# Strided attention on one core: stores of one head parity from every second partition, for two groups at a time

## The chip, the cores and the metric

The kernel runs on one core of a Trainium2 chip. The metric is the device time in microseconds (us), the median over several executions. The profile is one further execution; its instruction times count from the start of its span.

## The reference

Inputs Q, K, V are fp32 of shape (8, 12, 1024, 64): batch, heads, sequence, head dimension. Every query attends to only 16 keys, the positions 0, 64, 128 ... 960.

```python
attend_positions = np.arange(0, seq, stride)          # stride 64: 16 positions
scores = einsum('bhqd,bhkd->bhqk', q, K[:, :, attend_positions]) / sqrt(dim)
weights = exp(scores - max(scores)); weights /= sum(weights) + 1e-10
result = einsum('bhqk,bhkd->bhqd', weights, V[:, :, attend_positions])
```

The output has the shape of V. So Q (25.2 MB) is read once, the output (25.2 MB) is written once, and little else moves.

## The kernel before, in words

The 96 heads are cut into 24 groups of four heads. A group is 1 MiB of Q and 1 MiB of output. All DMA transfers are issued on SP's queue by the helper `_copy` (L26 to L41); nearly every one therefore carries the line L35.

Loads. `load(g)` brings a group of Q into a tile `qn` of 128 partitions with 8 KiB each (32 query rows of one head). The first two groups are read as 128 rows of 8 KiB, all later ones as 32 rows of 32 KiB (L93 to L96). There are QBUFS = 8 such tiles, so eight loads are issued at the start, with K and V among them.

Work on one group `g`, spread over the engines and over several turns of the main loop:

- `cast` (L199, POOL): Q to bf16, three groups ahead.
- `transpose` (L203, DVE): 32 by 32 blocks of 4-byte pairs, two groups ahead.
- `scores` (L210, PE): four matmuls into one PSUM bank of 128 partitions by 512; then two exps on ACT (L221) write the weights into `w`, 64 partitions each. A head parity `a` (0 or 1) has its keys on 64 of the partitions and its queries in half of the 128 columns of each of the eight blocks of `w`; the other half of its columns stays zero from a memset at the start. One group ahead.
- `values` (L191, POOL): the values of the group's keys, spread by a mask, with four columns that make the sums of the weights.
- `outputs(g, c)` in three parts of 3, 2 and 3 blocks (L235, PE): each matmul takes one block of `w` as its weights, so a column of `w` becomes a partition of the output. DVE takes the reciprocal of the sums (L243); parts of 3 blocks are scaled by DVE (L245), the part of 2 is copied by ACT (L247) and scaled by POOL (L248). They write the tile `out_sb`, 128 partitions of 8 KiB. There are OBUFS = 9 of them.
- `store(g)`: one transfer, 128 reads of 8 KiB, each written as two pieces of 4 KiB.

The layout of `out_sb` before: partitions 0 to 63 hold the even heads of the group, partitions 64 to 127 the odd ones. Each partition holds 16 query rows of each of two heads, and row j of the 128 goes to byte offset 4096 j of the group for one head pair, and 512 KiB further on for the other.

Order. The program is written out by hand (a manual schedule; each engine keeps the order of the program text). In turn g of the main loop come `ahead(g)`, the three `outputs`, now and then a piece of preparing keys and values, then `store(g)` and `load(g + 8)`. SP goes through its queue in order: a store waits for the group's last writes to `out_sb`, and the load behind it waits with it. A transfer is counted on one of eight DMA semaphores in turn, and before a transfer is issued SP also waits until the one eight places earlier on the queue has landed. A tile `out_sb` is written again only when the stores that read it have landed; a tile `qn` is loaded again only when its cast is done.

Of the kernel before, what the change touches and what calls it, by code (L numbers as in the profile page):

```python
# [11 lines left out]
FP32 = mybir.dt.float32  # L12
# [7 lines left out]
def _ap_with(ap: bass.AP, new_ap, extra_offset: int = 0) -> bass.AP:  # L20
    return dataclasses.replace(
        ap, ap=[list(p) for p in new_ap], offset=ap.offset + extra_offset
    )


def _copy(nc, out: bass.AP, in_: bass.AP):  # L26

    sides = [
        mybir.BassSymbolicTensorAccessPattern(
            ap=side.ap, dtype=side.dtype, bass_ap=side,  # L30
            is_dma=True, for_custom_bir_dma=True,
        )
        for side in (in_, out)
    ]
    return nc.sync.add_instruction(  # L35
        mybir.InstDMACopy(
            name=nc.get_next_instruction_name(), engine=mybir.EngineType.SP,
            ins=sides[:1], outs=sides[1:], queue="qSPDynamicHW",
            mode="Copy",
        )  # L40
    )  # L41
# [9 lines left out]
def kernel(  # L51
# [10 lines left out]
    B, H, S, D = Q.shape  # L62
# [3 lines left out]
    P = 128  # L66
    HG = 4
    NG = B * H // HG
    NC = NG // 2
    SD = S * D  # L70
    KW = P + NK
    assert B * H == NG * HG and S == 1024 and D == 64 and NK == 16
    QBUFS = 8
    OBUFS = 9

    const = ctx.enter_context(tc.tile_pool(name="const", bufs=1))
    qn_pool = ctx.enter_context(tc.tile_pool(name="qn", bufs=QBUFS))
    out_pool = ctx.enter_context(tc.tile_pool(name="outsb", bufs=OBUFS))
    qb_pool = ctx.enter_context(tc.tile_pool(name="qb", bufs=2))
# [13 lines left out]
    def load(g):  # L93
        qn[g] = qn_pool.tile([P, 32 * D], FP32, name="qn", tag="qn")
        n = P if g < 2 else 32
        _copy(nc, qn[g], _ap_with(Q, [[HG * SD // n, n], [1, HG * SD // n]], g * HG * SD))  # L96
# [3 lines left out]
    nc.sync.dma_start(v_raw, _ap_with(V, kv_src))  # L100
    for g in range(1, QBUFS):
        load(g)
# [12 lines left out]
    for c in range(2):  # L115
        for a in range(2):
            for e in range(2):
                nc.gpsimd.tensor_copy(  # L118
                    out=perm_v[:, c, a, :, e], in_=id_v[:, c, :, a]
# [5 lines left out]
    for i in range(3):  # L125
# [7 lines left out]
        out=slot_i, in0=iota_p, scalar1=4, scalar2=3,  # L133
# [6 lines left out]
        out=s_sel, in0=col4, scalar1=slot_f, scalar2=None, op0=ALU.is_equal  # L140
# [15 lines left out]
    def key_rows(m):  # L156
        part = slice(4 * m, 4 * m + 4)
        nc.scalar.copy(k_bf[:, part], k_raw[:, part])  # L158
        nc.vector.transpose(  # L159
            k_r[:, part].rearrange("p n d -> p (n d)").bitcast(I32),  # L160
            k_bf[:, part].rearrange("p n d -> p (n d)").bitcast(I32),
        )


    def keys(m, c):
        for s in range(4):
            src, dst, col = 32 * (2 * c + s % 2), 32 * (2 * (s % 2) + s // 2), NK + 32 * s
            op = nc.vector.tensor_copy if m == 0 and s >= 2 else nc.scalar.copy
            op(  # L169
                k_t[dst : dst + 32, 8 * m + c : 8 * m + 8 : 2, :, col : col + NK],  # L170
                k_r[src : src + 32, 4 * m : 4 * m + 4].rearrange(
                    "p n (a k f) -> p a n f k", a=2, f=2
                )[:, s // 2],
            )


    def value_rows(n):
        for c in range(2):
            vp = psum_sc.tile([P, NC // 2, D], FP32, name="vp", tag="sc")
            nc.tensor.matmul(  # L180
                vp, lhsT=perm_v[:, c].rearrange("p a b e k -> p (a b e k)"),
                rhs=v_bf[:, 6 * n : 6 * n + 6], start=True, stop=True,
            )
            nc.vector.tensor_copy(out=v_rep[:, 6 * n : 6 * n + 6, c], in_=vp)  # L184

    qb, qt, wt, vb, rec, out_sb = {}, {}, {}, {}, {}, {}


    def values(g):
# [15 lines left out]
    def scores(g):  # L205
        sc = psum_sc.tile([P, 512], FP32, name="sc", tag="sc")
        q = qt[g]
        for e in range(2):
            for f in range(2):
                nc.tensor.matmul(  # L210
                    sc, lhsT=k_t[:, g, f, NK * (1 - e) : NK * (1 - e) + P],
                    rhs=_ap_with(
                        q, [q.ap[0], [D, 8], [16 * D, 2], [2, 32]],
                        extra_offset=8 * D * e + f,
                    ),
                    start=e + f == 0, stop=e + f == 2,
                )
        w = wt[g] = w_bufs[g % 3]
        for a in range(2):
            wa = w[64 * a : 64 * a + 64]  # L220
            nc.scalar.activation(  # L221
                out=_ap_with(wa, [wa.ap[0], [P, 8], [1, 2], [2, 32]], extra_offset=64 * a),
                in_=sc[64 * a : 64 * a + 64].rearrange("p (t x q) -> p t x q", t=8, x=2),
                func=AF.Exp, bias=0.0, scale=scale,
            )


    def outputs(g, c):
        if c == 0:
            out_sb[g] = out_pool.tile([P, 4, 8, D], FP32, name="out_sb", tag="out_sb")  # L230
            rec[g] = rec_pool.tile([P, 8, 4], FP32, name="rec", tag="rec")
        i0, n = ((0, 3), (3, 2), (5, 3))[c]
        ps = psum_o.tile([P, 3, 512], FP32, name="o_ps", tag="o")
        for i in range(n):
            nc.tensor.matmul(  # L235
                ps[:, i, 0 : 4 * D + 4], lhsT=wt[g][:, i0 + i], rhs=vb[g],
                start=True, stop=True,
            )
        r = rec[g][:, i0 : i0 + n]
        o = ps[:, 0:n, 0 : 4 * D].rearrange("p i (s d) -> p i s d", s=4)  # L240
        to = out_sb[g][:, :, i0 : i0 + n].rearrange("p s i d -> p i s d")
        by = r.unsqueeze(3).to_broadcast([P, n, 4, D])
        nc.vector.reciprocal(r, ps[:, 0:n, 4 * D : 4 * D + 4])  # L243
        if n == 3:
            nc.vector.tensor_tensor(out=to, in0=o, in1=by, op=ALU.mult)  # L245
        else:
            nc.scalar.copy(to, o)  # L247
            nc.gpsimd.tensor_tensor(out=to, in0=to, in1=by, op=ALU.mult)  # L248

    def store(g):  # L250
        o = out_sb[g]
        _copy(
            nc,
            _ap_with(out, [[16 * D, P], [2 * SD, 2], [1, 16 * D]], g * HG * SD),
            _ap_with(o, [o.ap[0], [1, 1], [1, 32 * D]]),
        )

    key_rows(0)
# [2 lines left out]
    keys(0, 0)  # L261
    transpose(0)
    scores(0)
    keys(0, 1)
    nc.vector.tensor_copy(out=v_bf, in_=v_raw)
# [5 lines left out]
    def ahead(g):  # L271
        if g + 2 < NG:
            transpose(g + 2)
        if g + 1 < NG:
            scores(g + 1)
        if g + 2 < NG:
            values(g + 2)
        if g + 3 < NG:
            cast(g + 3)

    for g in range(NG):
        if g > 0:
            ahead(g)
        for c in range(3):
            outputs(g, c)
        if g == 0:
            ahead(g)
        if g in (1, 5):
            key_rows(g // 4 + 1)
        if g in (2, 3, 6, 7):  # L290
            keys(g // 4 + 1, g % 4 - 2)
        if g == 4:
            value_rows(1)
        store(g)
        if g + QBUFS < NG:
            load(g + QBUFS)
# [1 line left out]
_INS = ['Q', 'K', 'V', 'stride']  # L298
_OUTS = [((8, 12, 1024, 64), 'float32')]
# [30 lines left out]
```

The softmax here doesn't subtract the row's maximum and nothing guards it: scores larger than these inputs give would overflow.

## Time and profile before

| What | Value |
|---|---|
| Median of 7 runs | 129.84 us (128.76 to 131.09) |
| The profiled execution's own time | 129.36 us |
| Its span in the profile | 127.6 us |
| Busy: DVE, POOL, PE, ACT | 95.6, 90.2, 69.3, 57.5 us |
| Granted TensorE clock, mean | 0.829 |
| Stores: median time from issue to landing | 9.5 us |
| Loads: the same | 11.6 us |
| Exp (L221), 64 x 512, each | 736 ns, 48 times |
| Copy by ACT (L247), 128 x 512, each | 585 ns, 24 times |
| Scale by DVE (L245), 128 x 768, each | 957 ns, 48 times |
| Transpose by DVE (L203), each | 1232 ns, 24 times |

How to read it: the busy rows of the page cut the span into 40 slices of 3.19 us, and a digit is the busy share in tenths. The DMA row is the mean over the 16 DMA engines. In the view of waits, a line says which engine at which line waited for which work, how long in total, how many times, and the longest one. In the table of windows the columns are the stretch, its length, busy time (and number of instructions) of PE, PEld (weight loads), DVE, ACT and POOL, the granted clock, the DMA share and the GB/s moved. SPq is SP's queue, where DMA transfers are issued; packet records list every DMA packet with its bytes and duration.

### The profile page before, as it was taken

What the parts mean: (1) busy time and instruction counts of PE and PEld (TensorE: products, weight loads), DVE (VectorE), ACT (ScalarE), POOL (GpSimd) and SP (SyncE); (2) the same over time, 40 slices, a digit from 0 to 9 for tenths busy, and PEclk for the clock granted to TensorE, in tenths of its full rate; (3) what the DMA queues carried; (4) which work ended last, traced back from release to release, by engine and by line L of the source; (5) the groups of instructions that cost most, each with busy time, mean ns of one, the idle gap of its engine ahead of it and who ended that gap; (6) DMA issues with size and microseconds to landing.
All of it is one profiled execution on the core that took longest, in us unless ns stands there. A gap on an engine that the chain in (4) does not pass through costs nothing.

```text
span 127.6 us, 1150 instructions
## 1 busy us (share of the span) xinstructions
PE 69.3 (54%) x292; PEld 30.9 (24%) x292; DVE 95.6 (75%) x167; ACT 57.5 (45%) x96; POOL 90.2 (71%) x89
## 2 busy tenths in 40 slices
PE   0005267796344796756545964367665656864200
PEld 0001032243112342313312432124332323331000
DVE  6947557778898677898889788988799887988400
ACT  4110613548781457584454354463555536452100
POOL 8952489976898376798889868988888888533300
PEclk9999999999997555699995599996579985599555
DMA  2999999998998999989999989989989999999990
GB/s 65 343 324 501 401 421 431 390 472 349 493 421 362 493 385 406 488 352 431 460 388 436 470 380 454 467 362 467 457 357 495 403 388 418 424 429 426 418 388 26
DMA packets 7910, 51.19 MB, mean 401 GB/s; under 512 B 3872, under 2 KB 3872, under 8 KB 3872
## 3 DMA queue, kind: packets, MB, share of 16 engines
q1 hardware_dynamic: 7904, 51.12, 96.6%
q8 instruction: 2, 0.03, 0.1%
q14 instruction: 4, 0.03, 0.1%
HBM read 25.95 MB, written 25.17 MB: 400 GB/s over the span
## 4 chain that ended last, share of the span: by engine, by line
DVE 50%; PE 17%; DMA 13%; issue 10%; POOL 2%; SPq 1%; ACT 0%
DVE out_sb L245 31%; PE o_ps L235 13%; DVE qt L203 11%; DMA qn<-in_Q_dram 7%; DVE rec L243 7%; DMA out_dram<-out_sb 6%; PE sc L210 4%; POOL qb L199 1%; POOL v L191 1%; DVE v_rep L184 1%; SPq L35 1%; ACT out_sb L247 0%; SPq L100 0%; DVE k_r L159 0%; SPq L98 0%
## 5 line engine op out<-in xcount | busy, mean ns | idle before, releaser
L235 PE MATMUL o_ps<-v,w 128*128 128x260 bf16 x192 | 40.7, 339 | 34.1 <-DVE out_sb L245 32.6
L221 ACT ACTIVATE w<-sc 64x512 bf16<-64x512 f32 x48 | 35.3, 736 | 32.2 <-PE sc L210 30.4
L199 POOL CAST qb<-qn 128x2048 bf16<-128x2048 f32 x24 | 45.3, 1889 | 4.1 <-DMA qn<-in_Q_dram 4.1
L245 DVE TENSOR_TENSOR out_sb<-o_ps,rec 128x768 f32<-128x768 f32 x48 | 46.0, 957 | 1.7
L210 PE MATMUL sc<-qt,k_t 128*128 128x512 bf16 x96 | 35.2, 502 | 13.3 <-DVE qt L203 11.8
L248 POOL TENSOR_TENSOR out_sb<-out_sb,rec 128x512 f32<-128x512 f32 x24 | 25.0, 1042 | 23.0 <-ACT out_sb L247 22.9
L235 PEld LDWEIGHTS <-w 128*128 128x128 bf16 x192 | 19.2, 116 | 62.3 <-DVE out_sb L245 46.0
L203 DVE STREAM_TRANSPOSE qt<-qb 128x1024 int32<-128x1024 int32 x24 | 29.6, 1232 | 4.9 <-POOL qb L199 4.9
L243 DVE RECIPROCAL rec<-o_ps 128x12 f32<-128x12 f32 (+1 forms) x72 | 15.3, 213 | 16.2 <-PE o_ps L235 16.1
L247 ACT COPY out_sb<-o_ps 128x512 f32<-128x512 f32 x24 | 14.0, 585 | 23.4 <-issue 11.4
L191 POOL TENSOR_TENSOR v<-mask,v_rep 128x256 bf16<-128x256 bf16 x24 | 16.0, 669 | 2.3 <-DVE v_rep L184 2.3
L210 PEld LDWEIGHTS <-k_t 128*128 128x128 bf16 x96 | 11.2, 117 | 24.9 <-issue 12.0
L169 ACT COPY k_t<-k_r 32x128 bf16<-32x128 bf16 x20 | 5.9, 295 | 2.0 <-DVE k_r L159 1.7
L129 POOL MEMSET k_t<- 128x4608 bf16 x1 | 3.9, 3937 | 0.0
L180 PE MATMUL vp<-v_bf,perm_v 128*128 128x384 bf16 x4 | 1.5, 413 | 2.5 <-DVE v_rep L184 2.5
L158 ACT CAST k_bf<-k_raw 128x256 bf16<-128x256 f32 x3 | 1.2, 405 | 3.3 <-DMA k_raw<-in_K_dram 3.2
L139 DVE TENSOR_SCALAR s_sel<-col,slot_f 128x4 bf16<-128x4 int16 x1 | 2.5, 2546 | 0.1
L184 DVE CAST v_rep<-vp 128x384 bf16<-128x384 f32 x4 | 2.1, 543 | 0.6 <-PE vp L180 0.6
L123 DVE MEMSET k_t<- 128x1152 uint32 x1 | 1.0, 1018 | 1.0 <-PEq L311 1.0
L158 ACT ACT_TABLE_LOAD x1 | 1.3, 1283 | 0.7 <-PEq L311 0.7
L127 DVE MEMSET w<- 128x512 uint32 x3 | 1.5, 485 | 0.2
L118 POOL COPY perm_v<-identity 128x32 bf16<-128x32 bf16 x8 | 1.2, 210 | 0.0
(16 smaller groups left out, 4.8 us busy)
## 6 DMA issues: line engine op xcount, KB each, us to landing
qn<-in_Q_dram SPq DMA_DIRECT2D x24, 1024.0 KB, 11.6
out_dram<-out_sb SPq DMA_DIRECT2D x24, 1024.0 KB, 9.5
k_raw<-in_K_dram SPq DMA_DIRECT2D x1, 384.0 KB, 4.5
v_raw<-in_V_dram SPq DMA_DIRECT2D x1, 384.0 KB, 7.5
```

The costliest lines, as they stand in the source:

```text
L129: nc.gpsimd.memset(k_t[:, 8:NG], 0.0)
L169: op(k_t[dst : dst + 32, 8 * m + c : 8 * m + 8 : 2, :, col : col + NK], k_r[src : src + 32, 4 * m : 4 * m + 4].rearrange("p n (a k f) -> p ...
L191: nc.gpsimd.tensor_tensor(out=vb[g][:, 0 : 4 * D].rearrange("p (s d) -> p s d", s=4), in0=mask, in1=v_rep[:, g // 2, g % 2].unsqueeze(1).t ...
L199: nc.gpsimd.tensor_copy(out=qb[g], in_=qn[g])
L203: nc.vector.transpose(qt[g].bitcast(I32), qb[g].bitcast(I32))
L210: nc.tensor.matmul(sc, lhsT=k_t[:, g, f, NK * (1 - e) : NK * (1 - e) + P], rhs=_ap_with(q, [q.ap[0], [D, 8], [16 * D, 2], [2, 32]], extra_ ...
L221: nc.scalar.activation(out=_ap_with(wa, [wa.ap[0], [P, 8], [1, 2], [2, 32]], extra_offset=64 * a), in_=sc[64 * a : 64 * a + 64].rearrange( ...
L235: nc.tensor.matmul(ps[:, i, 0 : 4 * D + 4], lhsT=wt[g][:, i0 + i], rhs=vb[g], start=True, stop=True,)
L243: nc.vector.reciprocal(r, ps[:, 0:n, 4 * D : 4 * D + 4])
L245: nc.vector.tensor_tensor(out=to, in0=o, in1=by, op=ALU.mult)
L247: nc.scalar.copy(to, o)
L248: nc.gpsimd.tensor_tensor(out=to, in0=to, in1=by, op=ALU.mult)
```

## The change

Two groups share one output tile of 128 partitions with 16 KiB each (`out_2`), with four such tiles. The exps write the columns of `w` so that the two head parities alternate: column 2r + a instead of 64a + r. With that, output partition 2r + a holds parity a. A store takes one parity of both groups: every second partition, 64 reads of 16 KiB, each written as four pieces of 4 KiB to four heads; for one head the 64 pieces follow each other, 256 KiB in a row. After every second group two such stores are issued, each followed by a load. There are ten tiles for Q instead of eight, so ten loads are issued at the start. The amount of data and the number of transfers stay as they are.

```diff
-    QBUFS = 8
-    OBUFS = 9
+    QBUFS = 10
+    OBUFS = 4
...
             nc.scalar.activation(
-                out=_ap_with(wa, [wa.ap[0], [P, 8], [1, 2], [2, 32]], extra_offset=64 * a),
+                out=_ap_with(wa, [wa.ap[0], [P, 8], [2, 2], [4, 32]], extra_offset=a),
...
     def outputs(g, c):
         if c == 0:
-            out_sb[g] = out_pool.tile([P, 4, 8, D], FP32, name="out_sb", tag="out_sb")
+            if g % 2 == 0:
+                out_2[g // 2] = out_pool.tile(
+                    [P, 2, 4, 8, D], FP32, name="out_sb", tag="out_sb"
+                )
+            out_sb[g] = out_2[g // 2][:, g % 2]
...
-    def store(g):
-        o = out_sb[g]
+    def store(n, a):
+        o = out_2[n][a : P : 2]
         _copy(
             nc,
-            _ap_with(out, [[16 * D, P], [2 * SD, 2], [1, 16 * D]], g * HG * SD),
-            _ap_with(o, [o.ap[0], [1, 1], [1, 32 * D]]),
+            _ap_with(
+                out, [[16 * D, 64], [2 * SD, 4], [1, 16 * D]],
+                2 * n * HG * SD + a * SD,
+            ),
+            _ap_with(o, [o.ap[0], [1, 1], [1, 64 * D]]),
         )
...
-        store(g)
-        if g + QBUFS < NG:
-            load(g + QBUFS)
+        if g % 2 == 1:
+            for a in range(2):
+                store(g // 2, a)
+                if g - 1 + a + QBUFS < NG:
+                    load(g - 1 + a + QBUFS)
```

More of the change, by code (lines that the diff above doesn't have):

```diff
@@ L184, in value_rows @@
             nc.vector.tensor_copy(out=v_rep[:, 6 * n : 6 * n + 6, c], in_=vp)
-    qb, qt, wt, vb, rec, out_sb = {}, {}, {}, {}, {}, {}
+    qb, qt, wt, vb, rec, out_sb, out_2 = {}, {}, {}, {}, {}, {}, {}
     def values(g):
```

## The prediction

> **What bounds the kernel now.** I read the slices of the page first, then the waits of SP's queue, then the last microseconds cut into windows, because the change moves nothing but stores, loads and the layout that feeds them.
>
> ```profile
> DVE  6947557778898677898889788988799887988400
> ...
> POOL 8952489976898376798889868988888888533300
> ...
> DMA  2999999998998999989999989989989999999990
> ...
> q1 hardware_dynamic: 7904, 51.12, 96.6%
> ```
>
> From the second slice to the end the 16 DMA engines are all but full: 51.12 MB, 96.6% of the span. DVE and POOL are nearly as full. So there are two candidates, and the totals do not say which one ends last.
>
> ```profile
> SPq L35 <- DVE out_sb L245: 84.3, 24, 11.3
> ...
> SPq L325 <- DMA out_dram<-out_sb: 5.0, 1, 5.0
> ```
>
> This is SP's queue: all 24 stores were waited for, each until VectorE wrote the last piece of its group (L245). A store leaves the moment its group is computed. In the timeline of SP's queue those issues stand at 20.74, 27.86, 32.14 ... 76.44, 80.53, 84.61, 88.70 us (4.09 us a group), then 93.08 for group 16, and the last at 120.5.
>
> ```profile
> 116.00:120.00 4.00, 1.73 (x8) 0.61 (x8) 3.08 (x7) 0.64 (x2) 1.95 (x2) 0.77 1.01 424
> 120.00:121.20 1.20, 0.00 (x0) 0.00 (x0) 0.39 (x1) 0.00 (x0) 0.13 (x1) 0.50 1.02 430
> 121.20:121.80 0.60, 0.00 (x0) 0.00 (x0) 0.00 (x0) 0.00 (x0) 0.00 (x0) 0.50 0.92 382
> 121.80:124.00 2.20, 0.00 (x0) 0.00 (x0) 0.00 (x0) 0.00 (x0) 0.00 (x0) 0.50 1.00 417
> 124.00:125.00 1.00, 0.00 (x0) 0.00 (x0) 0.00 (x0) 0.00 (x0) 0.00 (x0) 0.50 0.36 148
> 125.00:126.00 1.00, 0.00 (x0) 0.00 (x0) 0.00 (x0) 0.00 (x0) 0.00 (x0) 0.50 0.08 33
> ```
>
> The last two columns are the DMA share and GB/s. Compute ends at 120.4. The share dips to 0.92 at 121.2 to 121.8: some engines had nothing left until the last store's packets came, about 1.25 us after its issue. It falls off at 124.2, where by the packet records 13 engines are done; three laggards run to 125.7, and the last landing is 126.1. So the two bounds meet at the end: DMA is full for 120 us, yet the last store already starts on engines that were about to be idle. A gain in either one alone is worth almost nothing, and more work held back until the last group is done is paid in full.
>
> [...] what I see is 425 GB/s with all 128. [...] loads after the first two have 32 source rows and run at the same rate as 128-row stores (packet records: median 311 ns for 8 KiB stored, about 1219 ns for 32 KiB loaded), so a row count other than 128 has not upset the spread. [...]
>
> **The change part by part.**
>
> Engine programs. As built, PE, DVE, ACT and POOL hold the same instructions in the same order; only SP's order changes. The sum below is therefore about when transfers leave.
>
> Exp writes (L221). 48 instructions of 736 ns now step 8 bytes instead of 4. I take no change. Upper bound: copies of 256 and 512 elements take 405 and 585 ns, so about 225 ns is fixed and 511 ns of an exp goes by element; doubled, an exp takes 1247 ns, 1.02 us more per group. ACT then works 2 x 1.25 + 0.585 = 3.1 us of 4.09, still below the group. The cover is that scores run a group ahead: in the timeline the exps of one group end at 102.5 and the next group's first output matmuls follow near 105. If the cover failed, it would cost up to 1 us a group. Lower bound: nothing gained, ACT is not waited for.
>
> Store packets. 3072 reads of 8 KiB become 1536 of 16 KiB. 8 KiB cost 311 ns alone and 1219 / 4 = 305 ns inside a 32 KiB load. If 16 KiB reads reached that, 6 ns x 3072 / 16 engines = 1.15 us of DMA time goes. I credit 0.6 us of DMA time and 0 of the end, since the end will be set by compute (next). [...]
>
> Start. Loads 8 and 9 now go ahead of any store; the first store leaves at 27.9 (group 1) instead of 20.7. In the trace load 7 lands by 26.9; two more loads carry the queue to about 31.8, and the store's packets would be there at 27.9 + 1.25 = 29.1. Cover 2.7 us; cost 0.
>
> Middle. A pair puts 4.19 MB (9.9 us) on the queue every 8.2 us, so the queue falls behind and stays filled, as before. Each instruction waits on one of eight DMA lanes until the transfer eight places earlier has landed; SP holds loads behind a blocked store, and each is still issued well ahead. Load 23 moves from behind store 15 (88.7) to behind pair 6 (80.5), place 39 instead of 41 on the queue, and lands some 5 us earlier, near 101. That removes the 0.47 us for which the cast at 106.55 waited on it: I credit 0.2 us.
>
> Buffers. A pair's first write now waits for both stores of the pair four before. The tightest is pair 11: the second store of pair 7 is at place 42 and lands at about 109; group 22 writes from 114. Slack 5 us, cost 0; it would take a store some 10% slower to use it up. The doubled DMA waits on DVE, ACT and POOL pass at once; behind them are the reciprocal and the next transposes, as before.
>
> End. This is what costs. Before: last issue 120.5, packets 1.25 us later, 1.05 MB in 2.47 us, about 0.4 us until landed, plus the laggards' 1.4 us: 126.1. After: the last group lets 2.10 MB go. When it is issued the engines have run dry, the laggards too: without the last two stores even they are done at 125.7 - 4.9 = 120.8. So 120.5 - 0.2 + 1.25 + 4.93 + 0.4 = 126.9, which is 0.8 us later. Nothing covers this; the loads are long over.
>
> Sum: 0 + 0 + 0 - (in the end term) + 0.8 = +0.8 us on the profiled span of 127.6, whose own run took 129.36. The median of the runs is 129.84; I add to that: 130.6, which is +0.6%.
>
> **The rivals.**
>
> Ports shared (slower). [...] Against: the row counts 32 and 128 both run at line rate. For: no 64-row transfer is in the trace. [...] at 10 to 30% longer stores, 5.9 to 17.8 us more than a full queue's 126.1, it gives 136 to 147. It decides from about 1 us of idle DMA at the end divided by 24 stores: 0.04 us a store, 2%.
>
> DMA is the real bound (faster). Then 16 KiB reads save up to 1.15 us: 128.7. For: 96.6% busy. Against: the dip at 121.2 and the exact 24 waits for VectorE. It would need compute to end 2 us earlier.
>
> Compute becomes slower. If the exp stride or a wait on out_sb reaches the DVE chain by 0.1 us a group, 24 groups make 2.4 us: 133. For: PE and DVE hand o_ps back and forth all along with no spare. Against: the slacks above.
>
> The end hidden. If pair 11 is computed 0.8 us earlier, or the engines finish more evenly than I think, the time stays at 129.8; this I count inside the forecast.
>
> **How the numbers follow.** Chances: forecast with its end of 0 to 1.5 us later, 0.66; ports shared 0.16; compute slower 0.12; DMA bound 0.06. One per cent (1.3 us) is about what a measurement of this kernel can tell from no change. The forecast's own range is 129.6 to 131.6: of its 0.66, 0.46 lies within 1%, 0.18 beyond on the slow side, 0.02 below. Ports add 0.15 and slow compute 0.07 to slower; the rest of these lies within; DMA bound gives 0.05 to faster. Slower 0.40, same 0.53, faster 0.07. The range of 129.2 to 136 takes in the forecast, the slow compute and the mild end of shared ports.
>
> **What would show it.** Right: the last stores issue near 120.5 again, about 1 us of low DMA share lies before their packets, and they land at about 127; SP still waits for L245, twelve times; 16 KiB packets take 611 to 622 ns. Wrong: packets of 16 KiB well above 650 ns (ports), exps clearly above 736 ns, waits on out_sb for DMA, or a last compute before 119.

## The result and the profile after

The changed kernel takes 131.34 us (median; 130.28 to 132.34) beside 129.52 us for the kernel before on the same chips. The ratio is 1.013, 95% interval 1.011 to 1.0149: 1.7 us slower (0.013 x 129.5). The forecast was +0.8 us, within 1% of before; the time lies in the range, but about half of the loss was not foreseen.

The profiled execution of the changed kernel took 132.34 us with a span of 130.3, at the top of its runs and 1.0 us above their median, so it shows where time goes, and how much is taken from the ratios.

The same rows of the page as before, then SP's queue in the view of waits:

```profile
DVE  6936557777888688898788987898879888867300
ACT  3110924969996499997699766897676977872100
POOL 8952489865976749796879987879878698223300
...
DMA  2999998999998998989999999999999999989194
...
q1 hardware_dynamic: 6368, 51.12, 95.3%
```

```profile
SPq L35 <- DVE out_sb L249: 79.1, 12, 15.7
SPq L335 <- DMA out_dram<-out_sb: 5.4, 1, 5.4
```

The DMA row is full to slice 37 and then shows a 1: a hole that the kernel before did not have. Twelve waits for VectorE stand where there were 24, one for each pair. The bytes are the same, the packets fewer (6368 against 7904), as 16 KiB reads should make it. And the ACT row, not shown before because nothing hung on it, is now at 9 in many slices; ACT's busy time went from 57.5 to 84.9 us. The group that did it is the exps; the second group is the copy behind them. First as they were before:

```profile
ACT  4110613548781457584454354463555536452100
...
L221 ACT ACTIVATE w<-sc 64x512 bf16<-64x512 f32 x48 | 35.3, 736 | 32.2 <-PE sc L210 30.4
...
L247 ACT COPY out_sb<-o_ps 128x512 f32<-128x512 f32 x24 | 14.0, 585 | 23.4 <-issue 11.4
```

And in the changed kernel:

```profile
L221 ACT ACTIVATE w<-sc 64x512 bf16<-64x512 f32 x48 | 62.8, 1308 | 24.5 <-PE sc L210 23.5
...
L251 ACT COPY out_sb<-o_ps 128x512 f32<-128x512 f32 x24 | 14.1, 585 | 5.7 <-DVE rec L247 5.0
```

An exp takes 1308 ns instead of 736. The copy takes what it took, but ACT's idle time ahead of it fell from 23.4 us to 5.7: ACT used to be free when a copy came up, and now the copy mostly has to wait for ACT.

The end of the changed kernel in windows (columns as in the prediction; the last two are DMA share and GB/s):

```profile
119.00:120.80 1.80, 0.99 (x5) 0.39 (x5) 1.31 (x4) 0.23 (x1) 0.32 (x1) 0.50 1.03 437
120.80:123.80 3.00, 0.52 (x3) 0.03 (x1) 1.19 (x2) 0.36 (x1) 1.04 (x1) 0.50 0.09 38
123.80:128.80 5.00, 0.00 (x0) 0.00 (x0) 0.00 (x0) 0.00 (x0) 0.00 (x0) 0.50 1.00 419
128.80:130.30 1.50, 0.00 (x0) 0.00 (x0) 0.00 (x0) 0.00 (x0) 0.00 (x0) 0.50 0.00 0
```

For 3.0 us the DMA engines have almost nothing to do (0.09), then they carry the last 2.1 MB in 5.0 us, and that is the end. The last piece of compute ends at 122.6 here, 120.4 before. So two things are visible: compute ends later, and what follows it is longer. How much of the 2.2 us between the two ends belongs to the single executions can't be read from them (in experiment 2, which came out as a repeat of the kernel before, compute ends at 121.4; in experiment 8, which puts both causes into that kernel, at 121.8). The experiments take the two things apart.

### The profile page after: what moved, and what is told of

The parts are those of the page before. It is cut to its first block, busy times and chain, and to the rows that moved or that the text cites. A ratio compares the mean times of both kernels' runs of the same rounds, so it can differ in the third digit from the quotient of the medians.

```text
span 130.3 us, 1125 instructions
## 1 busy us (share of the span) xinstructions
PE 71.3 (55%) x292; PEld 31.0 (24%) x292; DVE 95.8 (74%) x167; ACT 84.9 (65%) x96; POOL 90.0 (69%) x89
## 3 DMA queue, kind: packets, MB, share of 16 engines
q1 hardware_dynamic: 6368, 51.12, 95.3%
## 4 chain that ended last, share of the span: by engine, by line
DVE 55%; PE 18%; DMA 7%; issue 6%; ACT 4%; POOL 2%; SPq 1%; DVEq 0%; ACTq 0%
DVE out_sb L249 33%; DVE qt L203 14%; PE o_ps L239 14%; DVE rec L247 7%; DMA qn<-in_Q_dram 7%; PE sc L210 4%; ACT w L221 2%; POOL qb L199 1%; ACT out_sb L251 1%; DVE v_rep L184 1%; SPq L35 1%; POOL v L191 1%; SPq L100 0%; DVE k_r L159 0%; SPq L98 0%
## 5 line engine op out<-in xcount | busy, mean ns | idle before, releaser
L221 ACT ACTIVATE w<-sc 64x512 bf16<-64x512 f32 x48 | 62.8, 1308 | 24.5 <-PE sc L210 23.5
L239 PE MATMUL o_ps<-v,w 128*128 128x260 bf16 x192 | 41.4, 348 | 34.2 <-DVE out_sb L249 32.6
```

The costliest lines, as they stand in the source:

```text
L221: nc.scalar.activation(out=_ap_with(wa, [wa.ap[0], [P, 8], [2, 2], [4, 32]], extra_offset=a), in_=sc[64 * a : 64 * a + 64].rearrange("p (t ...
L239: nc.tensor.matmul(ps[:, i, 0 : 4 * D + 4], lhsT=wt[g][:, i0 + i], rhs=vb[g], start=True, stop=True,)
```

## The experiments

Ratios are to the kernel before, with 95% intervals. Theory at the outset: two causes, the long exp and the held-back last pair. Rivals: one of the two alone, or the 64-row stores themselves.

**1. The long exp alone (b_exp8).** The kernel before with one line of the change:

```diff
-                out=_ap_with(wa, [wa.ap[0], [P, 8], [1, 2], [2, 32]], extra_offset=64 * a),
+                out=_ap_with(wa, [wa.ap[0], [P, 8], [2, 2], [4, 32]], extra_offset=a),
```

> The kernel before, with only the exp writes of the change (every 8 bytes instead of every 4); the stores are those of before, so the rows of the two head parities come out in each other's places. Two-causes theory (the exp goes from 736 to about 1308 ns and holds up the ACT copy behind it, and the last pair's 2 MiB leave at once): exps of about 1308 ns, the ACT copy found waited for by PE, +0.7 us (0.4 to 1.2) against the kernel before. Tail-only theory (the longer exp is hidden, as the prediction said): exps of 1308 ns but no change, within 0.2 us. Exp-only theory: +1.7 us. DMA theory (the 64-row stores themselves are slower): no change.

Measured: 1.0044 (1.0016 to 1.0072), +0.6 us. The exps took 1308 ns, and the view of waits shows who felt it. The second line is the one to compare: in the kernel before, PE's weight loads waited for the ACT copy once, 0.5 us in all.

```profile
PE o_ps L235 <- DVE out_sb L245: 34.1, 24, 2.2
...
PEld L235 <- ACT out_sb L247: 5.1, 8, 1.4
```

So the long exp costs, about a third of the whole loss. Tail-only falls, exp-only too.

**2. The held-back store, first attempt (b_tail).** In the last turn `store(g - 1)` then `store(g)`, and none in the turn before:

```diff
-        store(g)
+        if g < NG - 2:
+            store(g)
+        if g == NG - 1:
+            store(g - 1)
+            store(g)
```

> The kernel before, with the store of group 22 held back until group 23 is done, so that 2 MiB leave after the last group; nothing else changed. Two-causes theory: the DMA engines run dry before it, +1.0 us (0.6 to 1.4) against the kernel before. Tail-only theory: +1.7 us. Exp-only and DMA theories: no change, within 0.2 us.

Measured: 0.9991 (0.9972 to 1.001). The edit did not do what it was meant to. SP's queue has the same order as before, and SP waits for each store's own data, so group 22's store left when group 22 was done (its last write ends at 118.15 us, the store is issued at 118.2; group 23 is done at 121.4), although the program text puts it in the next turn. The run is a repeat of the kernel before and says nothing on the tail.

**3. The held-back store, done properly (b_hold).** `store(g)` ahead of `store(g - 1)` in the last turn, so that the queue itself holds the earlier one.

> The kernel before, with group 23's store ahead of group 22's on SP's queue, so that the queue holds group 22's store until group 23 is done and 2 MiB really leave after the last group. Two-causes theory: two stores land about 6.6 us after the last group instead of 5.6, +1.0 us (0.6 to 1.4) against the kernel before. If the tail only costs where the exp has made the last group late: within 0.3 us of the kernel before.

Measured: 1.0069 (1.0039 to 1.0098), +0.9 us, with the exps at 736 ns. Its end in windows:

```profile
119.20:121.20 2.00, 0.00 (x0) 0.00 (x0) 0.80 (x1) 0.00 (x0) 0.55 (x1) 0.50 0.15 61
121.20:126.20 5.00, 0.00 (x0) 0.00 (x0) 0.00 (x0) 0.00 (x0) 0.00 (x0) 0.50 1.01 419
126.20:128.30 2.10, 0.00 (x0) 0.00 (x0) 0.00 (x0) 0.00 (x0) 0.00 (x0) 0.50 0.02 4
```

The hole and the 5.0 us block are there without any of the other edits: this is the tail that the prediction priced at +0.8.

**4. The tail taken out of the changed kernel (a_tail).** For the last pair, each group stores its two parities by itself (64 reads of 8 KiB, 0.5 MiB):

```diff
+        if g >= NG - 2:
+            for a in range(2):
+                store_one(g, a)
-        if g % 2 == 1:
+        elif g % 2 == 1:
```

> The changed kernel, with the stores of the last pair made per group again (each parity of one group, 0.5 MiB, 64 reads of 8 KiB), so that only 1 MiB is left after the last group; the exp writes stay as changed. Two-causes theory: 1.0 us less than the changed kernel, so +0.7 us (0.3 to 1.1) against the kernel before. Tail-only theory: as the kernel before. Exp-only and DMA theories: still +1.7 us.

Measured: 1.0019 (1.0002 to 1.0036). Beside the changed kernel's 1.013 that is 1.1%, or 1.4 us, less. The exps are still at 1308 ns, and now cost 0.2%.

```profile
119.00:120.80 1.80, 0.83 (x3) 0.28 (x3) 0.99 (x3) 0.58 (x1) 0.34 (x1) 0.50 1.04 437
120.80:123.80 3.00, 0.00 (x0) 0.00 (x0) 0.97 (x2) 0.00 (x0) 0.71 (x1) 0.50 0.96 399
123.80:125.60 1.80, 0.00 (x0) 0.00 (x0) 0.00 (x0) 0.00 (x0) 0.00 (x0) 0.50 1.03 428
```

The same stretch that stood at 0.09 is at 0.96. Group 22's stores fill it.

**5. Short exps in the changed kernel, by the matmul's order (a_mm).** Let PE produce the scores in the order in which `w` wants them:

```diff
-                        q, [q.ap[0], [D, 8], [16 * D, 2], [2, 32]],
+                        q, [q.ap[0], [D, 8], [2, 32], [16 * D, 2]],
...
-                out=_ap_with(wa, [wa.ap[0], [P, 8], [2, 2], [4, 32]], extra_offset=a),
+                out=_ap_with(wa, [wa.ap[0], [P, 8], [2, 64]], extra_offset=a),
```

> The changed kernel, with the same columns of w written in another order: the scores matmul reads Q in the order query row, then half, so that its PSUM columns stand in the order of the columns of w, and the exp writes every 4 bytes instead of every 8. Stores and pairing as changed; the output is the same. Two-causes theory: exps back near 736 ns if the distance between consecutive writes is what costs, and 0.7 us (0.4 to 1.2) less than the changed kernel, so +1.0 us against the kernel before. Tail-only theory: no change, +1.7 us. Exp-only theory: as the kernel before. If the matmul's reading order slows PE instead, L210 shows it above 507 ns.

Measured: 1.1043 (1.0987 to 1.1099), 13.5 us slower than before; a miss for all the theories, though the last sentence of the expectation names what happened:

```profile
L210 PE MATMUL sc<-qt,k_t 128*128 128x512 bf16 x96 | 56.4, 709 | 12.9 <-DVE qt L203 11.8 <-DVE v_rep L184 1.1
```

The exps came back (738 ns), but the matmul, whose moving operand (`rhs` in the kernel) now jumps 2 KiB (1024 bf16) between neighbouring columns, takes 709 ns on average instead of 507 in the changed kernel. Part of that is the granted clock, 0.695 against 0.845 on average. Between 20 and 30 us both traces have a clock of 1.00, so the four matmuls of a group can be compared there, the changed kernel first:

```profile
26.85 1.91 PE L210 MATMUL sc<-qt,k_t 128*128 128x512 bf16 x4
```

```profile
27.14 2.36 PE L210 MATMUL sc<-qt,k_t 128*128 128x512 bf16 x4
```

The reading order alone costs 0.45 us for four, about 110 of the 200 ns; the rest goes with the lower clock. The run shows that a 4-byte exp is short again, and nothing on the size of its effect.

**6. Short exps by ACT's own order (a_xq).** The same elements to the same places, only the loop order turned:

```diff
-                out=_ap_with(wa, [wa.ap[0], [P, 8], [2, 2], [4, 32]], extra_offset=a),
-                in_=sc[64 * a : 64 * a + 64].rearrange("p (t x q) -> p t x q", t=8, x=2),
+                out=_ap_with(wa, [wa.ap[0], [P, 8], [4, 32], [2, 2]], extra_offset=a),
+                in_=sc[64 * a : 64 * a + 64].rearrange("p (t x q) -> p t q x", t=8, x=2),
```

> The changed kernel, with each exp writing the same elements in another order: query row outside, half inside, so that consecutive writes are 4 bytes apart instead of 8, and ACT reads PSUM alternating between two places 128 bytes apart; matmuls, stores and pairing as changed; the output is the same. If the distance between consecutive writes is what costs: exps back near 736 ns, and 0.3 to 0.8 us less than the changed kernel, so +0.9 to +1.4 us against the kernel before. If ACT's cost is in the set of places and not in their order, or its PSUM reads now cost as much: exps at 1308 ns or more and +1.7 us.

Measured: 1.0057 (1.0034 to 1.0081), 0.9 us less than the changed kernel.

```profile
L221 ACT ACTIVATE w<-sc 64x512 bf16<-64x512 f32 x48 | 35.5, 740 | 30.2 <-PE sc L210 29.5
```

740 ns with the same set of places: what costs is the distance from one write to the next, not where the writes fall. What is left, 0.6%, agrees with the tail of experiment 3 (0.7%).

**7. Both causes taken out (a_xq_tail).** The edits of 4 and 6 together.

> The changed kernel with both suspected causes taken away: exp writes 4 bytes apart in the order query row, half; and the last pair stored per group, each parity by itself. What stays of the change: 64-row stores of 16 KiB from every second partition for the first 11 pairs, ten load tiles, pairing. Two-causes theory: within 0.3 us of the kernel before; a little faster (0.3 to 0.6 us) if the DMA time saved by 16 KiB reads reaches the end. DMA theory (the 64-row stores cost): still 0.5 us or more slower.

Measured: 0.9991 (0.9974 to 1.0007). What remains of the change, 16 KiB reads from every second partition, is worth nothing that can be measured, either way. This is also the best version of the changed kernel that was found; it does not beat the kernel before.

**8. Both causes put into the kernel before (b_both).** The edits of 1 and 3 together.

> The kernel before with the two suspected causes put in and nothing else of the change: exp writes every 8 bytes, and group 22's store held behind group 23's. No 64-row stores, no pairing, eight load tiles; the rows of the two head parities come out in each other's places. If the two causes are the whole of it: as the changed kernel, +1.3% (1.0 to 1.6%). If the rest of the change helps or hurts, the difference shows here: over 1.6% if 16 KiB stores had been helping, under 1.0% if they had been hurting.

Measured: 1.0151 (1.0113 to 1.0188), which takes in the changed kernel's 1.013. Together with 7 this closes the account: the two causes make the loss, and the rest of the change does not show.

**9. Neighbouring partitions instead of every second (a_half).** The changed kernel with the exp line of before and

```diff
-        o = out_2[n][a : P : 2]
+        o = out_2[n][64 * a : 64 * a + 64]
```

> The changed kernel with the layout of before: exp writes every 4 bytes into halves of the columns, so that one parity lies on 64 neighbouring partitions, and each store reads those 64 partitions (16 KiB each) instead of every second one; the output is the same. [...] as the changed kernel with short exps, +0.9 to +1.4 us against the kernel before.

Measured: 1.0717 (1.0665 to 1.0769), 9.3 us slower than before, with much scatter: its six runs lie between 137.8 and 143.6 us, 8 to 14 us above the kernel before. The price is real: far more than the +0.9 to +1.4 us expected, though far less than stores at twice their 2.47 us would cost (an estimate: 24 x 2.47 us = 59 us). Two rows of its page, where the loads have ended by slice 33 or so and only stores are left:

```profile
DMA  2999899989999989989999999999999999999980
GB/s 68 370 347 500 377 425 464 416 367 300 333 423 319 396 358 406 367 365 447 391 348 435 435 445 411 391 430 435 416 425 430 401 420 420 416 406 358 324 275 34
```

The DMA engines are busy throughout but move less in places: 300 to 333 GB/s in slices early on and 275 to 358 at the end. By the packet records a 16 KiB packet has the same median as in the changed kernel (615 against 616 ns), but some take up to 1638 ns, and the mean is 659 against 620; a load packet of 32 KiB takes 1305 against 1256. For 1536 and 704 packets on 16 engines that is an estimated 5.9 us of DMA time. What makes some packets long, and where the rest of the 9.3 us comes from, stays open. It is not that the stores are slow throughout and loads fill in for them: the last load packet ends at 108.6 us, and after that the stores, still each from 64 neighbouring partitions, go on at 413 and 406 GB/s for 10 us before they fall off to 380 and 344:

```profile
110.00:115.00 5.00, 2.24 (x11) 0.84 (x9) 3.72 (x7) 2.05 (x3) 3.43 (x4) 0.88 1.00 413
115.00:120.00 5.00, 3.14 (x15) 1.28 (x13) 3.20 (x8) 2.05 (x3) 1.25 (x2) 0.78 1.01 406
120.00:125.00 5.00, 0.83 (x3) 0.28 (x3) 1.89 (x4) 0.58 (x1) 1.04 (x1) 0.56 0.96 380
125.00:130.00 5.00, 0.00 (x0) 0.00 (x0) 0.00 (x0) 0.00 (x0) 0.00 (x0) 0.50 1.02 344
```

**10 and 11. How an exp's time goes with the distance of its writes (b_xq, a_exp16).** b_xq is the kernel before with experiment 6's loop order, which makes its writes neighbours (`[2, 32], [1, 2]`); a_exp16 is the changed kernel writing `[2, 4], [8, 16]`.

> The kernel before with each exp writing in the order query row, half, so that consecutive writes are 2 bytes apart; the output is the same. If an exp's time goes on falling with the distance of its writes: below 700 ns; if 4 bytes already is the fast case, or the alternating PSUM reads set the pace: about 736 ns. The time within 0.3 us of the kernel before either way, since a 736 ns exp holds nothing up.

> The changed kernel with the same elements of w written in steps of 16 bytes instead of 8 (the scores are read in the order they lie, so the rows inside a head come out permuted). If each write past a 4-byte step costs one fixed extra: exps about 1308 ns again. If it goes by the distance: about 2400 ns, and the kernel several us slower. If 16 bytes is past what counts and 8 was a special case: back near 736 ns.

Measured: b_xq 0.9988 (0.9965 to 1.0012); a_exp16, one execution, 169.18 us. The exp of b_xq first, that of a_exp16 second, each from its list of groups:

```profile
L221 ACT ACTIVATE w<-sc 64x512 bf16<-64x512 f32 x48 | 28.4, 592 | 32.6 <-PE sc L210 30.8 <-PE o_ps L235 1.1
```

```profile
L221 ACT ACTIVATE w<-sc 64x512 bf16<-64x512 f32 x48 | 117.4, 2447 | 9.3 <-PE sc L210 8.5
```

So 592, 736, 1308 and 2447 ns at 2, 4, 8 and 16 bytes. From 4 bytes on the time goes by the distance: 572 ns more for 4 bytes more, then 1139 for 8. a_exp16 takes the covering question to its end: PE's weight loads waited 40.4 us for the ACT copy (0.5 in the kernel before), and ACT is busy for 138.0 of the 167.0 us, more than any other engine.

## Why the prediction was half right

**The end: right.** "Nothing covers this", priced at 2.1 MB after the last group for 0.8 us. Put alone into the kernel before it costs 0.9 us (b_hold), and the hole, the 1.25 us until packets come and the 5.0 us block are in the windows as worked out. (Two of its readings are loose, and nothing hangs on them: DVE and POOL, "nearly as full" as the DMA engines, are busy for 75 and 71% of the span beside 96.6%; and of the engines counted as done at 124.2, most finish between 124.2 and 124.5.)

**Exp writes: wrong, and this is the step that failed.** It said "I take no change". The exp went from 736 to 1308 ns, a little past even the upper bound of 1247. That bound took 225 ns of an exp as fixed, worked out from two other kinds of copy; the exps' own times at 4 and 8 bytes leave 164 (736 less the 572 that doubling the distance adds). The value itself, no change, was the author's estimate: the trace of the kernel before holds no exp whose writes lie 8 bytes apart, so nothing in it showed what one takes.

**The cover: named, but for the wrong instruction.** The step asked whether the exps would be done before the matmuls that read `w`. They are, with one exception that costs time, group 1, where in b_exp8 the first weights come 0.8 us later and the first matmul 0.4 us later than in the kernel before (23.89 for 23.53):

```profile
23.89 0.78 PEld L235 LDWEIGHTS <-w 128*128 128x128 bf16 x5 [1.02 <-ACT w L221]
```

It did not ask what stands behind the exps on ACT. That is the copy of a group's middle part, which holds one of the two PSUM tiles `o_ps`. The turn of group 22 in the changed kernel, from its timeline (start, length, engine, line):

```profile
114.97 2.63 ACT L221 ACTIVATE w<-sc 64x512 bf16<-64x512 f32 x2 [1.31 <-PE sc L210]
...
116.77 0.20 DVE L247 RECIPROCAL rec<-o_ps 128x8 f32<-128x8 f32 x1
...
117.62 0.58 ACT L251 COPY out_sb<-o_ps 128x512 f32<-128x512 f32 x1
...
118.26 0.35 PEld L239 LDWEIGHTS <-w 128*128 128x128 bf16 x3 [1.00 <-ACT out_sb L251]
```

The copy could start at 116.97, when the reciprocal ends (where ACT is free it starts within 0.1 us of that, as in the next turn: 120.54 and 120.57); the exps hold ACT until 117.60; the copy runs to 118.20, and only then can PE start on the next group, having waited 1.00 us. A turn of the kernel before, for comparison (its timeline, group 17): the copy follows the reciprocal, which ends at 95.49, without a wait worth speaking of, since the exps ended at 95.05.

```profile
93.56 1.49 ACT L221 ACTIVATE w<-sc 64x512 bf16<-64x512 f32 x2 [1.92 <-PE sc L210]
...
95.29 0.20 DVE L243 RECIPROCAL rec<-o_ps 128x8 f32<-128x8 f32 x1
...
95.57 0.59 ACT L247 COPY out_sb<-o_ps 128x512 f32<-128x512 f32 x1 [0.52 <-POOL qb L199]
```

The full price named for a failed cover, "up to 1 us a group", would be some 24 us. It was 0.6 us in all (experiment 1). PE met the late copy only in a few turns (8 weight loads, 5.1 us of waits in b_exp8), and what was lost did not add up: by the timelines of SP's queue, b_exp8's store of group 4 leaves at 42.0 us, against 40.3 and 40.8 in two traces of the kernel before (before, b_tail), but that of group 6 at 51.2, against 51.4 and 51.2. What gives the time back in between was not tested. That the missed cover cost so little was luck: the prediction had it at nothing or at up to a full microsecond a group, and its sum was off by only 0.9 us in good part because the truth lay near nothing.

**Two bounds that meet: right, and it explains the sum.** Alone, the exp costs 0.44% and the tail 0.69%, 1.13% added up; together 1.30% (changed kernel) or 1.51% (b_both). On the changed kernel's stores the exp alone costs 0.19% and the tail alone 0.57%. The intervals allow plain addition for the first pair and hardly for the second (at most 0.36 + 0.81 = 1.17 against at least 1.10). It fits that the end is the later of the DMA queue and the last group, and the traces bear this out in part. In the four with a held-back pair (b_hold, a_xq, b_both and the changed kernel) the last packet ends 6.4 us after the last compute, whether that is at 119.7 or at 122.6: whatever compute loses is paid in full. In those without one that distance lies between 4.4 us (a_tail) and 6.1 (b_exp8); in the kernel before it is 5.3. In a_tail compute ends 1.4 us later than before and the last packet only 0.5, and in b_tail, the repeat of before, 1.0 and 0.5: there the busy queue took most of the delay up. In b_exp8 it did not (0.6 and 1.3 later). These are single traces, so how much is absorbed stays open.

**Start, middle, buffers: right.** No engine waits for a store to free an output tile in the view of waits of the changed kernel; DMA stays full until slice 37; the packets of the last load end at 102.9 (foreseen near 101). SP's wait for the transfer eight places earlier on the queue is in the trace at the start: loads 8 and 9 are issued at 9.72 and 12.20 us, and the transfers eight places before them have landed at 9.71 and 12.18.

**Store packets: right.** 16 KiB take 616 ns (median) against 2 x 311: 6 ns for 1536 packets over 16 engines is 0.6 us of DMA time, as credited, and 0 of it reaches the end (a_xq_tail).

**The rivals.** "Ports shared" stood for stores that take longer; the cause in its name was the author's estimate, and no trace or run shows it. Slower stores: not so; 616 ns for 16 KiB is a little under twice the 311 of 8 KiB (622), so a store of 64 rows from every second partition takes no longer for its bytes. Stores from 64 neighbouring partitions did cost time, 9.3 us in a_half, for a reason that the runs leave open. Slow compute was the rival that came true in part, by the very exp stride it names, at 0.6 us instead of 2.4.

## What to carry to other kernels

When an operation may get longer, look for what stands behind it on its own engine and which buffer that instruction gives back; the reader of its output is only half of the question (in b_exp8 PE's weight loads waited 5.1 us for the copy behind the exps, 0.5 before). A layout change that seems free on the writing side should be priced by the distance between consecutive writes (here on ACT, bf16: 736 ns at 4 bytes, 1308 at 8), and turning the loop order may bring the time back (1308 to 740 ns in a_xq) without moving a single element. Larger transfers that wait for more work before they leave were paid for at the end, where no later work covered them (0.9 us in b_hold): keep the last few small.

## What the runs showed of the hardware that was not expected

- An exp from PSUM to bf16 in SBUF (64 x 512) took 592, 736, 1308 and 2447 ns when consecutive writes lay 2, 4, 8 and 16 bytes apart (b_xq, the kernel before, the changed kernel, a_exp16). Reading PSUM in two alternating places 128 bytes apart cost nothing beside it (740 ns in a_xq against 736).
- Four matmuls (512 columns, bf16) whose moving operand alternates between two places 2 KiB apart took 2.36 us at a granted clock of 1.00, where steps of 4 bytes took 1.91 (a_mm and the changed kernel).
- Stores from 64 neighbouring partitions made the kernel 7.2% slower (6.7 to 7.7; a_half), those from every second partition, with the same tail and short exps, 0.6% (a_xq). Yet with no load under way such stores still moved 406 to 413 GB/s for 10 us.
- SP issued a store as soon as its own data were ready: moved later in the program text it left no later (118.2, b_tail); behind a store that waits it left 4.0 us after its own data were written (b_hold).
